# Last norm of a two-layer decoder step: part of its scaling on GpSimd, one tile's on ScalarE, and the samples' last weights taken one product earlier

## The chip, the cores and the metric

The kernel is one program on one core of a Trainium2 chip. The metric is the device time of one execution in microseconds. The engines are TensorE (PE in the profile; PEld is its weight load), VectorE (DVE), ScalarE (ACT), GpSimd (POOL) and SyncE (SP, which only issues transfers); 16 DMA engines move data, whoever issues the transfer.

## The reference

One inference step of a two-layer decoder: a gated linear attention layer and a differential attention layer, each followed by a squared-ReLU feed-forward block, with a layer norm behind every residual sum. There are 1024 new prompt tokens (16 meta tokens go ahead of them) and 8 running sequences with one token each, the "samples". Width 1024, hidden width 4096, all float32.

```
def layer_norm(x, g, b):
    mu = jnp.mean(x, axis=-1, keepdims=True)
    xc = x - mu
    var = jnp.mean(xc * xc, axis=-1, keepdims=True)
    return xc * lax.rsqrt(var + LN_EPS) * g + b
def post_norm(x, f, g, b):
    return layer_norm(DEEPNORM_ALPHA * x + f, g, b)
def sq_relu_mlp(x, w1, w2):
    h = jax.nn.relu(x @ w1)
    return (h * h) @ w2
# the last step of layer 1; y_prompt is x_p without its 16 meta rows, y_sample is x_s
x_p = post_norm(x_p, sq_relu_mlp(x_p, mlp_w1[1], mlp_w2[1]), ln_mlp_g[1], ln_mlp_b[1])
x_s = post_norm(x_s, sq_relu_mlp(x_s, mlp_w1[1], mlp_w2[1]), ln_mlp_g[1], ln_mlp_b[1])
```

## The kernel before

Only the end of the kernel matters here: the feed-forward block of the second layer (`mlp1`) and the norm behind it (`normalize`, `last`).

The 1024 prompt tokens are 8 tiles of 128 rows, held in `Y` (tile t is `Yt[:, t, :]`). The block runs over four groups `g` of 1024 hidden units. Each group has an up part (x times w1) and a down part (hidden times w2), and each part multiplies 2x2 blocks by Strassen's scheme with seven products, numbered 1 to 7. The last group's down part takes its products in the order 1, 5, 6, 7, 4, 3, 2. Each float32 product is three matmuls on a high and a low part: `XH` and its low half (left operand, split by ACT at L202 and VectorE at L203), `whi` and `wlo` (weights, split by ACT at L1528 and GpSimd at L1529). A product is four tiles of 12 matmuls of 512 columns (L206 to L208), into the PSUM buffers `axt` and `mmt`. VectorE adds each result into `RP` or `Y` (`down_tile`, L1600). Operands of the next product are prepared during tile 2 of the present one. Where a product's weight is a sum of two blocks, SP loads the first and GpSimd issues an adding transfer of the second on top (L1525, L1527). Weight slabs of 128x512 go through the tile pools `rw` (five buffers) and `raw` (two), and a fixed buffer `RW`.

The samples' tokens are multiplied beside this. Where a raw weight block is needed, `beside` multiplies a slab with `hs` (the samples' hidden values) into one of two PSUM accumulators (L1547), four slabs for each of four blocks; a slab that the product itself does not have raw is loaded once more (L1533). `beside.quarter` says which block belongs to which product. When all are done, `samples_out` adds residuals and norms the samples (`s_ln`, L667 to L688: sums by TensorE, the rest by VectorE, logarithm and exponential by ACT at L679 and L680), transposes back (L1482) and stores `y_sample`.

The last products finish Y: product 7 and 4 tiles 4 to 7, products 3 and 2 tiles 0 to 3. `normalize` takes each half tile's statistics on VectorE (L990, L994), raises the variance to -1/2 on GpSimd (L999), and ACT scales and shifts the tile in place (L1005). Then `last` applies the norm's scale row `fg` and shift row `fb` (both in the tile called XR):

- Tiles 0, 1 and 4 to 7: VectorE multiplies by `fg` (L1453). The shift rows have been written to the output earlier (L1651, from SP), and GpSimd issues a store of 512 KB that adds to them (L1454).
- Tiles 2 and 3: no ACT. VectorE does each half in two steps, (y - mean) * fg (L1458) and y * rstd + fb (L1459), and SP stores the half, 256 KB, directly (L1460).

The source sets dependences only; a scheduler writes each engine's instruction order when the program is built, and each engine runs its own in that order and waits at semaphores. So an instruction that waits holds everything behind it on its engine.

Of the kernel before, what the change touches and what calls it, by code (L numbers as in the profile page):

```python
# [16 lines left out]
ALU = mybir.AluOpType  # L17
# [5 lines left out]
D = 1024  # L23
# [91 lines left out]
def hybrid_step(ctx, tc, A, dbg=None, upto=9):  # L115
    nc = tc.nc
    V, S, G, TE = nc.vector, nc.scalar, nc.gpsimd, nc.tensor
# [867 lines left out]
    def normalize(steps, stats, done, last=None):  # L985

        st, mv, rs = stats
        half = set()
        for t, j in steps:
            V.bn_stats(st[:, t, j, :], Yt[:, t, j * 512 : (j + 1) * 512])  # L990
            if t not in half:
                half.add(t)
                continue
            V.bn_aggr(mv[:, t, :], st[:, t])  # L994
            if t % 2 == 0 and not last:
                continue
            ts = slice(t if last else t - 1, t + 1)
            V.tensor_scalar(rs[:, 0, ts], mv[:, ts, 1], EPS, None, ALU.add)
            steps_g.append(G.tensor_tensor(rs[:, 0, ts], rs[:, 0, ts], mhalf[:, : ts.stop - ts.start], op=ALU.pow).ins)  # L999
            if last and t in (2, 3):  # L1000
                last(t, mv, rs)
                continue
            V.scalar_tensor_tensor(rs[:, 1, ts], mv[:, ts, 0], -1.0, rs[:, 0, ts], ALU.mult, ALU.mult)
            for x in range(ts.start, ts.stop):
                S.activation(Yt[:, x, :], Yt[:, x, :], AF.Identity, bias=rs[:, 1, x : x + 1], scale=rs[:, 0, x : x + 1])  # L1005
            if last:
                last(t, mv, rs)
            if t % 4 == 3:
                done(t // 4)
# [401 lines left out]
    def rawt():  # L1411
        return rwp.tile([P, 512], F32, name="rw")
# [36 lines left out]
    def last(t, mv, rs):  # L1449

        y, out = Yt[:, t, :], A["y_prompt"][0, t * P : (t + 1) * P, :]
        if t not in (2, 3):
            V.tensor_tensor(y, y, fg, op=ALU.mult)  # L1453
            nc.gpsimd.dma_start(out, y, accum_op=ALU.add)  # L1454
            return
        for h in range(2):
            c = slice(512 * h, 512 * h + 512)
            V.scalar_tensor_tensor(y[:, c], y[:, c], mv[:, t, 0:1], fg[:, c], ALU.subtract, ALU.mult)  # L1458
            V.scalar_tensor_tensor(y[:, c], y[:, c], rs[:, 0, t : t + 1], fb[:, c], ALU.mult, ALU.add)  # L1459
            dma(out[:, c], y[:, c])  # L1460
# [48 lines left out]
    def weight_operand(terms, quarter, side=None):  # L1509

        hi, lo = (wsp.tile([P, 2048], F32R, name=n).rearrange("p (k n) -> p k n", n=512) for n in ("whi", "wlo"))
        run = terms[0] == "run"

        def src(q, k):
            w, r0, c0 = quarter(*q)
            return w[r0 + k * P : r0 + (k + 1) * P, c0 : c0 + 512]

        for k in range(4):
            if run or (len(terms) > 1 and terms[-1] != "new"):
                t = RW[:, k, :]  # L1520
            else:
                count[1] += 1
                t = wrp.tile([P, 512], F32, name="raw") if count[1] % 7 in (0, 3) else rawt()
            if not run:
                loads.append(dma(t, src(terms[0], k)).ins)  # L1525
            if len(terms) > 1:
                nc.gpsimd.dma_start(t, src(terms[1], k), accum_op=ALU.add)  # L1527
            S.copy(hi[:, k, :], t)  # L1528
            G.tensor_tensor(lo[:, k, :], t, hi[:, k, :].bitcast(F32), op=ALU.subtract)  # L1529
            if side:  # L1530
                if terms != [side.quarter]:
                    t = rawt()
                    dma(t, src(side.quarter, k))  # L1533
                side(k, t)
        return hi, lo

    w1, w2 = A["mlp_w1"][1], A["mlp_w2"][1]
# [1 line left out]
    def operands(g, up, i):  # L1539
        if up:  # L1540
            left = weight_operand(UP_W[i], lambda h, k: (w1, 512 * k, 1024 * g + 512 * h))
            right = chip_operand(UP_X[i], lambda k, c: xr(c)[:, 4 * k : 4 * k + 4, :], TH, RX)
            return left, right

        def beside(k, t):
            r, u = beside.quarter
            TE.matmul(acc[u][k * TS : (k + 1) * TS, :], hs[:, 4 * r + k, :], t, start=g == 0 and i in (1, 3), stop=g == 3 and r == 1)  # L1547


        beside.quarter = ({1: (0, 0), 3: (1, 1), 7: (0, 1), 2: (1, 0)} if g < 3 else {1: (0, 0), 5: (0, 1), 6: (1, 0), 7: (1, 1)}).get(i)  # L1550
        left = chip_operand(DOWN_H[i], lambda c, k: HF[:, 4 * k : 4 * k + 4, c, :512], 512, XF[0][:, : 4 * TH] if g == 3 and i == 7 else RX)
        right = weight_operand(DOWN_W[i], lambda k, u: (w2, 1024 * g + 512 * k, 512 * u), beside if beside.quarter else None)
        return left, right

    def hidden(h, c, m):
# [57 lines left out]
    def mlp1():  # L1613
# [6 lines left out]
        for at, (g, up, i) in enumerate(seq):  # L1620
            now = nxt
            if not up and i == 1:
                if g == 0:
                    beta = alpha_row(A["ln_mix_b"][1:2], ALU.add)
                else:
                    for _ in range(2):
                        next(beta, None)
            for t in range(4):
                if t == 2 and at + 1 < len(seq):
                    nxt = operands(*seq[at + 1])  # L1630
                if up:
# [12 lines left out]
            if g == 3 and not up and i == 7:  # L1644
                samples_out()
            if g == 3 and up and i == 7:
                for x, nm in ((fg, "g"), (fb, "b")):
                    dma(x, A["ln_mlp_" + nm][1:2].broadcast_to([P, D]))
                with tc.issue_after(loads[-1]):
                    for t0, t1 in ((0, 2), (4, 8)):  # L1650
                        dma(A["y_prompt"][0, t0 * P : t1 * P], A["ln_mlp_b"][1:2].broadcast_to([(t1 - t0) * P, D]))  # L1651
                spare.extend(XF[0][:, 4 * TH + 512 * j : 4 * TH + 512 * (j + 1)] for j in range(4))

# [30 lines left out]
```

## Time and profile before

| | |
|---|---|
| runs (us) | 2838.25, 2839.62, 2833.88; median 2838.25 |
| span of the profiled execution (first to last instruction) | 2828.8 us |
| device time of the profiled execution | not among the times shown; the median is 9.45 us above the span |
| busy: PE, PEld, DVE, ACT, POOL | 2735.8, 2242.1, 1937.3, 1084.4, 1115.2 us |
| share of the span | 97%, 79%, 68%, 38%, 39% |
| granted TensorE clock, mean | 0.989 |
| DMA | 562.81 MB, mean 199 GB/s |

TensorE is busy 97% of the span, so a change far from TensorE can count only where TensorE waits or has finished. Busy shares are means over the whole span; the end of the kernel must be read by itself, from stretches of the timeline in microseconds since the span's start.

### The profile page before, as it was taken

The page shows a single profiled execution, that of the slowest core. Times are in us where ns is not written, and L with a number is a line of the kernel's source. Part 1 is how long each engine was busy: PE and PEld are TensorE (multiplying, and loading weights), DVE is VectorE, ACT ScalarE, POOL GpSimd, SP SyncE. Part 2 cuts the span into 40 slices and gives each one's busy share as a digit, 9 for nine tenths or more (in the row PEclk, how much of TensorE's full clock was granted, in tenths as well). Part 3 has the DMA queues.
Part 4 walks back from the last instruction along what each step waited for, and adds up shares of the span by engine and source line. Part 5 has one row for each costly group of instructions (what it writes and reads, how often), then busy time and mean ns, then how long its engine had stood idle before and what let it go on. Part 6 is the DMA issues. An engine that isn't in the chain of part 4 may idle for free. (4 is left out here: it accounts for less than half of the span.)

```text
span 2828.8 us, 52247 instructions
## 1 busy us (share of the span) xinstructions
PE 2735.8 (97%) x19849; PEld 2242.1 (79%) x19849; DVE 1937.3 (68%) x3045; ACT 1084.4 (38%) x2221; POOL 1115.2 (39%) x744
## 2 busy tenths in 40 slices
PE   8999989999999999999999999999999999999997
PEld 5866668997777777777798988777898889797985
DVE  4364462568887787778568730877548878978788
ACT  4323343252221222221242112777535546355553
POOL 1142112334344343434234322100026767677764
PEclk9999999999999999999999999999999999999999
DMA  5568751725898898988658995122144555555683
GB/s 197 193 218 272 265 187 50 249 92 166 287 345 301 313 357 294 342 312 316 239 184 306 357 370 166 54 68 65 39 120 94 115 129 116 132 120 117 134 190 86
DMA packets 272552, 562.81 MB, mean 199 GB/s; under 512 B 23510, under 2 KB 140316, under 8 KB 268204
## 3 DMA queue, kind: packets, MB, share of 16 engines
q1 hardware_dynamic: 253004, 522.75, 53.8%
q0 software_dynamic: 19296, 36.71, 8.1%
q8 instruction: 156, 2.56, 0.4%
q14 instruction: 96, 0.79, 0.1%
HBM read 533.00 MB, written 29.52 MB: 199 GB/s over the span
## 5 line engine op out<-in xcount | busy, mean ns | idle before, releaser
L194 POOL TENSOR_TENSOR wlo<-raw,whi 128x512 fp32r<-128x512 f32 x256 | 379.1, 1495 | 727.2 <-ACT whi L193 589.2
L207 PE MATMUL mmt<-wlo,XH 128*128 128x256 f32 (+1 forms) x1760 | 523.4, 299 | 1.3 <-POOL wlo L194 1.3
L206 PE MATMUL mmt<-whi,XH 128*128 128x256 f32 (+1 forms) x1760 | 523.1, 300 | 1.3 <-DVE ast L1244 0.9
L206 PE MATMUL mmt<-XH,whi 128*128 128x512 f32 (+1 forms) x1216 | 435.3, 359 | 6.8 <-DVE Y L967 3.0
L208 PE MATMUL mmt<-whi,XL 128*128 128x256 f32 x1536 | 433.1, 285 | 0.0
L208 PE MATMUL mmt<-XH,wlo 128*128 128x512 f32 (+1 forms) x1216 | 432.5, 356 | 0.0
L193 ACT CAST whi<-raw 128x512 fp32r<-128x512 f32 x256 | 153.3, 620 | 574.3 <-PE mmt L208 184.9
L857 DVE TENSOR_REDUCE sc<-pg 128x16 f32<-128x1024 f32 x256 | 308.3, 1211 | 70.4 <-POOL pg L856 67.9
L207 PEld LDWEIGHTS mmt<-wlo,XH 128*128 128x128 f32 x1760 | 332.5, 189 | 24.8 <-issue 11.8
L206 PEld LDWEIGHTS mmt<-whi,XH 128*128 128x128 f32 x1760 | 330.8, 189 | 24.6 <-issue 11.8
L207 PE MATMUL mmt<-XL,whi 128*128 128x512 f32 x768 | 306.8, 399 | 0.0
L856 DVE TENSOR_TENSOR pg<-pg,qb 128x1024 f32<-128x1024 f32 x192 | 261.2, 1367 | 65.2 <-DMA pg<-in_cache_k 52.8
L208 PEld LDWEIGHTS mmt<-whi,XL 128*128 128x128 f32 x1536 | 288.8, 189 | 6.5 <-issue 5.8
L206 PEld LDWEIGHTS mmt<-XH,whi 128*128 128x128 f32 x1216 | 230.0, 189 | 49.4 <-issue 7.6
L856 POOL TENSOR_TENSOR pg<-pg,qb 128x1024 f32<-128x1024 f32 x64 | 161.3, 2522 | 260.2 <-DMA pg<-in_cache_k 174.3
L208 PEld LDWEIGHTS mmt<-XH,wlo 128*128 128x128 f32 x1216 | 230.0, 189 | 36.6 <-issue 4.1
L206 PE MATMUL mmt<-whi,HH 128*128 128x512 f32 x512 | 204.7, 401 | 3.9 <-DVE Y L1081 3.6
L208 PE MATMUL mmt<-whi,HL 128*128 128x512 f32 x512 | 203.9, 398 | 0.0
L207 PE MATMUL mmt<-wlo,HH 128*128 128x512 f32 x512 | 203.4, 397 | 0.0
L1529 POOL TENSOR_TENSOR wlo<-rw,whi 128x512 fp32r<-128x512 f32 x92 | 156.5, 1737 | 81.6 <-ACT whi L1528 80.2
L1529 POOL TENSOR_TENSOR wlo<-RW,whi 128x512 fp32r<-128x512 f32 x96 | 169.7, 1798 | 47.3 <-ACT whi L1528 47.2
L207 PEld LDWEIGHTS mmt<-XL,whi 128*128 128x128 f32 x768 | 145.4, 189 | 37.2 <-issue 5.5
(431 smaller groups left out, 5673.8 us busy)
## 6 DMA issues: line engine op xcount, KB each, us to landing
pg<-in_cache_k SPq DMA_DIRECT2D x256, 512.0 KB
pg<-in_cache_v SPq DMA_DIRECT2D x256, 512.0 KB
raw<-in_mlp_w SPq DMA_DIRECT2D x164, 256.0 KB
swt<-in_mlp_w SPq DMA_DIRECT2D x32, 1024.0 KB
rw<-in_mlp_w SPq DMA_DIRECT2D x116, 256.0 KB
RW<-in_mlp_w POOLq DMA_DIRECT2D x96, 256.0 KB, 5.9
raw<-in_gla_w_in SPq DMA_DIRECT2D x48, 256.0 KB
swt<-in_gla_w_in SPq DMA_DIRECT2D x12, 1024.0 KB
```

The costliest lines, as they stand in the source:

```text
L193: S.copy(hi[:, c], raw)
L194: G.tensor_tensor(lo[:, c], raw, hi[:, c].bitcast(F32), op=ALU.subtract)
L206: TE.matmul(ps, ah, bh, start=first, stop=False)
L207: TE.matmul(ps, ah, bl, start=False, stop=False)
L208: return TE.matmul(ps, al, bh, start=False, stop=last)
L856: eng.tensor_tensor(pg, pg, qb, op=ALU.mult)
L857: return V.tensor_reduce(sc[:, n, :], pg.rearrange("p (h d) -> p h d", d=64), op=ALU.add, axis=AX.X).ins
L1529: G.tensor_tensor(lo[:, k, :], t, hi[:, k, :].bitcast(F32), op=ALU.subtract)
```

## The change

It does three things. Tiles 0 and 1: the multiplication by `fg` goes from VectorE to GpSimd, in two halves of 512 columns each. Tile 2 now goes the way of the other tiles: ACT scales and shifts it, VectorE multiplies it by `fg` in one piece, and GpSimd issues an adding store, so its output rows are filled with the shift row as well (three tiles instead of two in the first fill). Only tile 3 keeps the two-step form. And in the last group, the samples' block (1, 0) is taken beside product 5 (with block (0, 1)) instead of 6, and block (1, 1) beside 6 instead of 7; `samples_out` is written behind product 6 instead of 7.

```
-            if last and t in (2, 3):
+            if last and t == 3:
                 last(t, mv, rs)
                 continue
...
     def last(t, mv, rs):
         y, out = Yt[:, t, :], A["y_prompt"][0, t * P : (t + 1) * P, :]
-        if t not in (2, 3):
-            V.tensor_tensor(y, y, fg, op=ALU.mult)
+        if t != 3:
+            eng = G if t < 2 else V
+            for h in range(2 if t < 2 else 1):
+                c = slice(512 * h, 512 * h + 512) if t < 2 else slice(0, D)
+                eng.tensor_tensor(y[:, c], y[:, c], fg[:, c], op=ALU.mult)
             nc.gpsimd.dma_start(out, y, accum_op=ALU.add)
             return
...
             if side:
-                if terms != [side.quarter]:
-                    t = rawt()
-                    dma(t, src(side.quarter, k))
-                side(k, t)
+                for q in side.quarters:
+                    if terms != [q]:
+                        t = rawt()
+                        dma(t, src(q, k))
+                    side(k, t, *q)
...
-        beside.quarter = ({...} if g < 3 else {1: (0, 0), 5: (0, 1), 6: (1, 0), 7: (1, 1)}).get(i)
+        beside.quarters = ({...} if g < 3 else {1: [(0, 0)], 5: [(0, 1), (1, 0)], 6: [(1, 1)]}).get(i)
...
-            if g == 3 and not up and i == 7:
+            if g == 3 and not up and i == 6:
                 samples_out()
...
-                    for t0, t1 in ((0, 2), (4, 8)):
+                    for t0, t1 in ((0, 3), (4, 8)):
                         dma(A["y_prompt"][0, t0 * P : t1 * P], A["ln_mlp_b"][1:2].broadcast_to([(t1 - t0) * P, D]))
```

Three lines more in the file move later line numbers by 3 (L1547 becomes L1550, L1454 becomes L1457, the multiplication L1453 becomes L1456). What the scheduler makes of it, at three places. First SP's queue in the last group's down part; `rw` and `raw` are weight slabs, L1533 (now L1537) the slabs for the samples alone, L1525 (now L1528) those for the products. Before:

```order
L1533 DMA rw<-in_mlp_w 128x512 x4
L1525 DMA rw<-in_mlp_w 128x512
L1533 DMA rw<-in_mlp_w 128x512
L1525 DMA rw<-in_mlp_w 128x512
L1533 DMA rw<-in_mlp_w 128x512 x2
L1525 DMA rw<-in_mlp_w 128x512
L1525 DMA raw<-in_mlp_w 128x512
L1533 DMA rw<-in_mlp_w 128x512
L1525 DMA rw<-in_mlp_w 128x512 x6
```

and after:

```order
L1537 DMA rw<-in_mlp_w 128x512 x2
L1528 DMA raw<-in_mlp_w 128x512
L1537 DMA rw<-in_mlp_w 128x512 x8
L1528 DMA rw<-in_mlp_w 128x512 x6
L1528 DMA raw<-in_mlp_w 128x512
```

The samples' slabs all stand ahead of product 7's three `rw` slabs now, where they stood between and behind them.

Second, the end of GpSimd's queue (`brs` is the variance raised to -1/2, XR the row `fg`). Before:

```order
L1454 DMA out_y_prompt<-Y 128x1024
L999 TENSOR_TENSOR brs<-brs,mhalf 128x1
L1454 DMA out_y_prompt<-Y 128x1024
L999 TENSOR_TENSOR brs<-brs,mhalf 128x1 x3
L1454 DMA out_y_prompt<-Y 128x1024 x2
L999 TENSOR_TENSOR brs<-brs,mhalf 128x1
```

and after:

```order
L1457 DMA out_y_prompt<-Y 128x1024 x2
L999 TENSOR_TENSOR brs<-brs,mhalf 128x1 x2
L1456 TENSOR_TENSOR Y<-Y,XR_25166 128x512 x2
L999 TENSOR_TENSOR brs<-brs,mhalf 128x1
L1456 TENSOR_TENSOR Y<-Y,XR_25166 128x512 x2
L1457 DMA out_y_prompt<-Y 128x1024
L999 TENSOR_TENSOR brs<-brs,mhalf 128x1
L1457 DMA out_y_prompt<-Y 128x1024 x2
```

The four half multiplications stand ahead of tile 0's store, with the power of tile 2 between them; the power of tile 3 stands ahead of tile 1's store, and tile 2's store is last.

Third, the end of TensorE's queue: tiles 2 and 3 of product 2 and the samples' eight transposes. Before, the transposes come last:

```order
L206 MATMUL mmt<-whi,XH_86 128x512
L207 MATMUL mmt<-wlo,XH_86 128x512
L208 MATMUL mmt<-whi,XH_24059 128x512
L1482 MATMUL smt<-c_ident,sx 32x128 x8
L1680 UNCONDITIONAL_BRANCH
```

and after, they have 15 matmuls behind them, of which these are the first:

```order
L208 MATMUL axt<-whi,XH_24059 128x512
L1485 MATMUL smt<-c_ident,sx 32x128 x8
L206 MATMUL axt<-whi,XH_86 128x512
L207 MATMUL axt<-wlo,XH_86 128x512
L208 MATMUL axt<-whi,XH_24059 128x512
L206 MATMUL mmt<-whi,XH_86 128x512
```

The three matmuls that end tile 2, and all of tile 3, now follow the samples' transposes.

More of the change, by code (lines that the diff above doesn't have):

```diff
@@ L1543, in operands, with beside @@
             return left, right
-        def beside(k, t):
-            r, u = beside.quarter
+        def beside(k, t, r, u):
             TE.matmul(acc[u][k * TS : (k + 1) * TS, :], hs[:, 4 * r + k, :], t, start=g == 0 and i in (1, 3), stop=g == 3 and r == 1)
-        beside.quarter = ({1: (0, 0), 3: (1, 1), 7: (0, 1), 2: (1, 0)} if g < 3 else {1: (0, 0), 5: (0, 1), 6: (1, 0), 7: (1, 1)}).get(i)
+        beside.quarters = ({1: [(0, 0)], 3: [(1, 1)], 7: [(0, 1)], 2: [(1, 0)]} if g < 3 else {1: [(0, 0)], 5: [(0, 1), (1, 0)], 6: [(1, 1)]}).get(i)
         left = chip_operand(DOWN_H[i], lambda c, k: HF[:, 4 * k : 4 * k + 4, c, :512], 512, XF[0][:, : 4 * TH] if g == 3 and i == 7 else RX)
-        right = weight_operand(DOWN_W[i], lambda k, u: (w2, 1024 * g + 512 * k, 512 * u), beside if beside.quarter else None)
+        right = weight_operand(DOWN_W[i], lambda k, u: (w2, 1024 * g + 512 * k, 512 * u), beside if beside.quarters else None)
         return left, right
```

## The prediction

> **What bounds the kernel now.** I read the busy time by stage first, then what each engine waited for in the last 90 us, then the timeline of the engines that wait, and last what the DMA engines do while the results are stored. Before the last feed-forward stage nothing changes, so I look from 2740 us on. Each row of the first fence gives a stretch of the span, then the busy time (and instruction count) of PE, PE's weight load, DVE, ACT and POOL, the granted clock, the busy share of the 16 DMA engines, and GB/s.
>
> ```profile
> 2740.00:2760.00 20.00, 19.46 (x88) 13.62 (x87) 18.84 (x18) 4.98 (x7) 12.16 (x12) 1.00 0.80 184
> 2760.00:2780.00 20.00, 18.35 (x80) 13.79 (x79) 15.94 (x17) 9.26 (x14) 14.09 (x9) 1.00 0.22 76
> 2780.00:2800.00 20.00, 18.90 (x84) 15.05 (x83) 19.99 (x40) 7.60 (x9) 7.89 (x8) 1.00 0.17 26
> 2800.00:2811.00 11.00, 10.55 (x47) 8.28 (x45) 9.63 (x24) 1.48 (x3) 5.00 (x7) 1.00 0.73 117
> 2811.00:2822.00 11.00, 1.03 (x8) 0.70 (x8) 10.90 (x24) 3.31 (x4) 4.74 (x6) 0.69 0.54 99
> 2822.00:2828.80 6.80, 0.00 (x0) 0.00 (x0) 0.63 (x1) 0.00 (x0) 0.00 (x0) 0.50 0.73 198
> ...
> DVE XH L203 <- ACT XH L202: 7.4, 2, 5.0
> DVE Y L1453 <- ACT Y L1005: 1.4, 1, 1.4
> ...
> PE axt L206 <- DVE sz L1475: 1.1, 1, 1.1
> PE axt L206 <- DVE RP L1600: 1.0, 1, 1.0
> PE axt L207 <- POOL wlo L1529: 0.6, 1, 0.6
> PE smt L1547 <- DMA rw<-in_mlp_w: 0.5, 1, 0.5
> ```
>
> Up to 2811 TensorE is nearly full (it loses 1.1 + 1.0 + 0.6 + 0.5 = 3.2 us to waits); from 2780 VectorE is full as well; after 2811 only VectorE works; after 2822 only the DMA engines. The wait rows are all that these two engines had from 2740 on (us in total, times, longest). The next fence is the timeline: start, duration, engine, line, and in brackets the idle time before it and what ended it.
>
> ```profile
> 2762.36 0.62 ACT L1528 CAST whi<-rw 128x512 fp32r<-128x512 f32 x1 [8.00 <-DMA rw<-in_mlp_w]
> 2762.88 1.99 ACT L202 CAST XH<-HF 128x1024 fp32r<-128x1024 f32 x2
> ...
> 2763.96 1.46 DVE L203 TENSOR_TENSOR XH<-HF,XH 128x1024 fp32r<-128x1024 f32 x1 [5.02 <-ACT XH L202]
> ...
> 2803.12 0.67 DVE L1600 TENSOR_TENSOR Y<-Y,mmt 128x512 f32<-128x512 f32 x1
> ...
> 2806.52 1.23 DVE L1453 TENSOR_TENSOR Y<-Y,XR 128x1024 f32<-128x1024 f32 x1 [1.36 <-ACT Y L1005]
> ...
> 2821.22 1.41 DVE L1459 SCALAR_TENSOR_TENSOR Y<-Y,brs,XR 128x512 f32<-128x512 f32 x2
> ```
>
> The reader sees a chain of queues. ACT waits 8.00 us for the fourth weight slab of product 7; the split of the left operand stands behind it in ACT's queue; so VectorE sits idle for 5.02 us, and from 2763.96 to 2803.75 (39.8 us, until the last sum of product 3 is in Y) it never idles again. It has fallen behind TensorE there and stays behind until the end.
>
> **The change, part by part.** *Samples' weights one product ahead.* Loads 9 to 12 of the side products leave the stretch in which product 7's weights are loaded. I let product 7's weights come in time, and then ACT's split waits only for TensorE to have read the left operand's old half, some six matmuls into product 6's last tile.
>
> ```profile
> 2740.05 1.07 PE L1547 MATMUL smt<-rw,hs 128*32 128x512 f32 x8
> ...
> 2755.99 0.39 PE L208 MATMUL axt<-whi,XH 128*128 128x512 f32 x1
> ...
> 2799.04 0.40 PE L206 MATMUL axt<-whi,XH 128*128 128x512 f32 x1
> ...
> 2810.16 0.40 PE L208 MATMUL mmt<-whi,XH 128*128 128x512 f32 x1
> ```
>
> Tile 2 of product 6 ends at 2756.4 (the L208 row of 2755.99). One of the 16 side products, 1.07/4 = 0.27 us, now stands ahead of that place: 2756.65. Product 2, 48 matmuls, takes 2799.04 to 2810.39, or 0.236 us a matmul, so six take 1.4: 2758.05. ACT's split is half of 1.99, some 1.05: VectorE starts at 2759.1 where it started at 2763.96. That is a gain of 4.8 us; its bounds are 0 (the weights are late all the same) and 4.8. The eight loads of product 5's side work in five buffers are costed at nothing: the first of them that must wait for a buffer is used some 24 matmuls, 5.7 us, after it is freed, and a 256 KB load took 3.7 us. Without that cover TensorE would lose the difference, up to 3 us.
>
> ```profile
> 2755.77 0.33 SPq L1533 DMA_DIRECT2D rw<-in_mlp_w  x1
> ...
> 2759.47 1.04 PE L1547 MATMUL smt<-rw,hs 128*32 128x512 f32 x2 [0.54 <-DMA rw<-in_mlp_w]
> ```
>
> VectorE then has the same 39.8 us of work up to product 3's last sum, plus the samples' steps that now come before it: L686, 0.41 or less, and five small ones like L683, some 0.1 each where the next instruction starts before they end, 0.85 us in all (rows below). So 2759.1 + 39.8 + 0.85 = 2799.8, against 2803.75. The 1.36 us wait goes: the samples' logarithm, which held ACT's queue there, now stands before ACT's split for product 2.
>
> ```profile
> 2803.72 1.27 DVE L990 BATCH_NORM_STATS2 bst<-Y 128x6 f32<-128x512 f32 x2
> ...
> 2808.36 0.18 DVE L683 TENSOR_TENSOR sv__31477<-sv__31477,sy__31478 128x32 f32<-128x32 f32 x1
> ...
> 2810.64 0.41 DVE L686 TENSOR_TENSOR sz<-sz,sy__31478 128x256 f32<-128x256 f32 x1
> ...
> 2815.27 1.22 DVE L1453 TENSOR_TENSOR Y<-Y,XR 128x1024 f32<-128x1024 f32 x1
> ```
>
> *TensorE's queue.* The samples' eight transposes now stand before the last 15 matmuls. They wait for VectorE's last sample step, which comes two statistics (0.6 each) and two steps of 0.33 after product 3's last sum: 2801.8. TensorE, rid of its 3.2 us of waits but kept about 1 us by POOL's last split of product 2 (its ACT cast stands behind the samples' logarithm, which waits for VectorE), is there at about 2802.9. Cover: 1.1 us; beyond that every us of VectorE's delay is one of TensorE's. TensorE ends near 2807.7 instead of 2810.55, which is not on the path.
>
> *The last norm.* From 2801.8 VectorE multiplies tile 7 (1.14 us), adds and measures tiles 0 and 1 (four times 0.6, and 0.25 for two or three small steps like L683): tile 0's variance is there at 2805.6. Then POOL's power (0.55 to 0.6), VectorE's 0.1, ACT's scaling (half of 2.37): 2807.5. Here POOL takes over:
>
> ```profile
> 2796.76 2.27 POOL L1529 TENSOR_TENSOR wlo<-raw,whi 128x512 fp32r<-128x512 f32 x1
> 2798.99 1.29 POOL L1529 TENSOR_TENSOR wlo<-rw,whi 128x512 fp32r<-128x512 f32 x1
> ...
> 2800.84 1.68 POOL L1529 TENSOR_TENSOR wlo<-rw,whi 128x512 fp32r<-128x512 f32 x1
> ...
> 2810.82 1.18 POOL L999 TENSOR_TENSOR brs<-brs,mhalf 128x1 f32<-128x1 f32 x2 [1.89 <-DVE brs L998]
> ...
> 2812.16 2.37 ACT L1005 ACTIVATE Y<-Y,brs 128x1024 f32<-128x1024 f32 x2 [5.55 <-DVE brs L1003]
> ```
>
> POOL's queue is: two halves of tile 0, the power of tile 2, two halves of tile 1, and only then tile 0's store. No multiplication by POOL stands at this place in the trace; the nearest is its subtraction of the same shape, 1.29 (VectorE on sums and statistics) to 2.27 us (VectorE on subtractions of two SBUF tensors). I take 1.29 for tile 0 and 1.68 for tile 1, beside which VectorE has its L1461 steps: 2 x 1.29 + 0.6 + 2 x 1.68 = 6.55, so 2814.05. Bounds: 5.75 and 9.7. The Trainium skill, "SBUF — State Buffer", section "Who interferes with whom", says that a tensor_tensor of VectorE with both inputs in SBUF and a GpSimd instruction exclude each other for a whole instruction. The 2.27 us row agrees with it and the 1.29 us row, taken beside VectorE's sums out of PSUM, does not contradict it; by that rule tile 1's halves, beside L1461, would take 2.27 each, POOL would be through at 2815.2 and the gain found below would be 0 instead of 1.2 us.
>
> VectorE loses in this stretch two multiplications (2 x 1.14) and tile 2's four half steps (two take 1.41 or less, start to start 0.66 each), and gains tile 2's one (1.14): 3.8 us less. It ends near 2816, when POOL's power of tile 3 has come, instead of 2821.96. If the stores did not bind, that would be the gain.
>
> *The stores.* Rows by stretch, as in the first fence (an adding store alone, two of them, then the last six stores), and the stores on the queues:
>
> ```profile
> 2795.00:2800.00 5.00, 5.00 (x24) 4.03 (x23) 5.00 (x8) 1.56 (x2) 5.00 (x4) 1.00 0.67 105
> 2801.00:2808.00 7.00, 7.00 (x32) 5.68 (x31) 5.63 (x13) 1.48 (x3) 2.93 (x4) 1.00 0.90 153
> 2818.00:2827.20 9.20, 0.00 (x0) 0.00 (x0) 4.56 (x9) 0.00 (x0) 1.86 (x2) 0.50 0.99 228
> ...
> 2794.37 0.90 POOL L1454 DMA_DIRECT2D out_y_prompt<-Y  x1 [1.73 <-ACT whi L1528]
> ...
> 2816.78 0.89 POOL L1454 DMA_DIRECT2D out_y_prompt<-Y  x1 [2.29 <-DVE Y L1453]
> ...
> DMA to landing us min/median/max: 5.2/5.8/7.9
> ```
>
> One adding store of 512 KB occupies all 16 DMA engines for 0.67 x 5 = 3.35 us, two for 6.3; I take 3.2 each. The last stretch holds two adding and four direct stores: 9.1 us, so a direct half tile is (9.1 - 6.4) / 4 = 0.68. The DMA engines are full there, from 2818 to 2827.05: this is what ends the kernel. After the change three adding and two direct stores remain, 3 x 3.2 + 2 x 0.68 = 10.95 us, and they cannot start before POOL is through: 2814.05 + 0.85 from issue to first bytes + 10.95 = 2825.85. That is 1.2 us before 2827.05. The start moves from 2816.78 to 2814.05, but the work behind it grows by 1.85.
>
> **The sum.** The span would be 2827.6 against 2828.8. The device time of that one execution is not shown; the median of the three runs, 2838.25, is 9.45 above its span, and I keep that distance: 2837.0. Its bounds, with POOL at 5.75 or 9.7 and VectorE 1 us either way: 2835 to 2841.5. Whatever is within 0.2%, 5.7 us, I call the same, which is what runs spread over 5.7 us can tell.
>
> **Rivals.** (A) The stores overlap and only the last counts. POOL issues tile 2's store at 2815.9; with the shortest landing, 5.2, it ends at 2821.1, 5.95 us earlier: 2832.3. For it: VectorE really ends 6 us earlier. Against: two stores issued 2.3 us apart needed 6.3 us of full engines. (B) Slower: three adding stores queued at once do not overlap at all, and each takes its median landing, 5.8: 2814.05 + 17.4 + 1.36 = 2832.8, which is 5.75 later, 2844.0. It decides as soon as a queued store costs more than 3.6 us. For it: the longest landing, 7.9. Against: the same 6.3 us for two. (C) The first part does not do what it says: product 7's weights, or TensorE, stall elsewhere, and VectorE starts as late as before. Then POOL starts 4.8 us later and everything ends at 2830.65, 3.6 later: 2841.85. For it: DMA is 0.80 busy from 2740 to 2760 and the twelve loads crowd into what comes just before. Against: TensorE has 24 matmuls of cover.
>
> **How the numbers follow.** My sum 0.62, A 0.16, B 0.07, C 0.12, something unseen 0.03. The time is that of the sum, 2837.0. The range goes from A to just short of B, 2831.8 to 2843.0; the sum's own is 2835 to 2841.5. Faster by over 0.2%: A, which lies at that bound, and a little scatter, 0.16; slower: B and a little of C, 0.08; the rest 0.76.
>
> **What would show it.** Right: ACT's 8 us wait and VectorE's 5 us wait are gone; POOL's multiplications take 1.3 to 1.7 us and tile 0's store is issued near 2814; VectorE ends near 2816 but the DMA engines are full for about 11 us up to some 2 us before the end. Wrong: if the DMA engines idle between the three stores, or if VectorE still waits for ACT near 2760, or if TensorE stands at the samples' transposes for more than 2 us.

## The result, and the profile after

The changed kernel is slower. Its 13 runs have a median of 2844.58 us, those of the kernel before on the same chip 2837.18; the ratio is 1.0025 with a 95% interval of 1.0015 to 1.0036, or 7.4 us (4.3 to 10.2). The profiled execution took 2844.68 us with a span of 2842.7, so what lies around the span is 1.9 us; in the runs on record it is 1.7 to 2.5 us.

Both traces must first be put on one clock. But for the one tile more that is filled with the shift row, the code ahead of the last group's down part is the same in both, yet its first 128x512 matmul of product 1 starts at another time. From the timeline of before, and then of after (start, duration, engine, line):

```profile
2722.07 0.39 PE L206 MATMUL axt<-whi,XH 128*128 128x512 f32 x1
```

```profile
2727.70 0.39 PE L206 MATMUL axt<-whi,XH 128*128 128x512 f32 x1
```

5.63 us of the 13.9 between the spans were there before the parts that I want to compare. I call this matmul's start zero, and give times from it as "at 41.9" from here on. The end of the span is at 106.7 before and at 115.0 after: 8.3 us, and that agrees with the 7.4 of the medians. Over all the profiles below, zero itself lies anywhere from 2721.8 to 2737.7; that is the spread of the runs, and a difference of a few us between two spans means nothing without this step.

The timeline after, the rows that answer to those of before:

```profile
2765.21 0.62 ACT L1531 CAST whi<-rw 128x512 fp32r<-128x512 f32 x1 [4.07 <-DMA rw<-in_mlp_w]
2766.79 0.62 ACT L1531 CAST whi<-rw 128x512 fp32r<-128x512 f32 x1 [0.96 <-DMA rw<-in_mlp_w]
2768.71 1.05 ACT L202 CAST XH<-HF 128x1024 fp32r<-128x1024 f32 x1 [1.29 <-PE mmt L207]
2769.79 1.23 DVE L203 TENSOR_TENSOR XH<-HF,XH 128x1024 fp32r<-128x1024 f32 x1 [0.45 <-ACT XH L202]
...
2814.47 0.68 DVE L1603 TENSOR_TENSOR Y<-Y,mmt 128x512 f32<-128x512 f32 x1
...
2821.77 1.24 ACT L1005 ACTIVATE Y<-Y,brs 128x1024 f32<-128x1024 f32 x1 [3.35 <-DVE brs L1003]
...
2823.09 2.49 POOL L1456 TENSOR_TENSOR Y<-Y,XR 128x512 f32<-128x512 f32 x2 [1.02 <-ACT Y L1005]
2825.54 0.55 POOL L999 TENSOR_TENSOR brs<-brs,mhalf 128x1 f32<-128x1 f32 x1
2826.05 2.48 POOL L1456 TENSOR_TENSOR Y<-Y,XR 128x512 f32<-128x512 f32 x2
2828.47 0.86 POOL L1457 DMA_DIRECT2D out_y_prompt<-Y  x1
...
2830.81 1.40 DVE L1462 SCALAR_TENSOR_TENSOR Y<-Y,brs,XR 128x512 f32<-128x512 f32 x2
```

The long waits are gone, ACT's 8.00 us and VectorE's 5.02. But VectorE's split for product 7 starts at 2769.79, which is at 42.09, where it started at 41.89: what was waited for by ACT is now waited for elsewhere. Product 3's last sum ends at 87.45 instead of 81.72. Tile 0's store is issued at 100.77 instead of 94.71. The end of the span by stretches (busy PE, PEld, DVE, ACT, POOL, the granted clock, DMA share, GB/s):

```profile
2822.00:2828.00 6.00, 0.00 (x0) 0.00 (x0) 4.95 (x11) 3.25 (x4) 4.97 (x6) 0.80 0.19 37
2828.00:2830.00 2.00, 0.00 (x0) 0.00 (x0) 2.00 (x3) 0.61 (x1) 2.00 (x3) 0.50 0.29 25
2830.00:2839.60 9.60, 0.00 (x0) 0.00 (x0) 2.21 (x3) 0.00 (x0) 1.86 (x3) 0.50 1.01 210
2839.60:2842.70 3.10, 0.00 (x0) 0.00 (x0) 0.00 (x0) 0.00 (x0) 0.00 (x0) 0.50 0.03 10
```

For 6 us the DMA engines do a fifth of what they could, while GpSimd multiplies; from 2830 they are full for 9.6 us; then 3.1 us pass in which next to nothing is busy (1.75 before). The full stretch near the end was predicted, but for its place on the clock.

Where TensorE lost its time is in the samples' matmuls. After (before, the rows were `x8`, `x8`, `x6`, `x2`; a slab leaves two records, so eight are the four slabs of a block):

```profile
2733.35 1.92 PE L1550 MATMUL smt<-rw,hs 128*32 128x512 f32 x10
2740.73 1.05 PE L1550 MATMUL smt<-rw,hs 128*32 128x512 f32 x2
2743.29 1.04 PE L1550 MATMUL smt<-rw,hs 128*32 128x512 f32 x2
2744.93 1.05 PE L1550 MATMUL smt<-rw,hs 128*32 128x512 f32 x2
2750.04 1.05 PE L1550 MATMUL smt<-rw,hs 128*32 128x512 f32 x4
2751.45 1.04 PE L1550 MATMUL smt<-rw,hs 128*32 128x512 f32 x2
2753.32 1.04 PE L1550 MATMUL smt<-rw,hs 128*32 128x512 f32 x2
```

One slab alone (`x2`) takes 1.05 us; four in a row took 1.07. They write 32 partitions each, in four different quarters of the accumulator. The Trainium skill, "TensorEngine Tiling (Array Packing)", section "Tiling Modes", says that with 32 columns the array works as four independent tiles; the two rows, 1.07 for four and 1.05 for one, agree with it. Slabs that come one at a time use one tile of the four, so eight groups (the `x10` row holds a group of four and a slab by itself) now stand ahead of product 6 where there were two, and product 6 starts at 31.33 instead of 24.63.

### The profile page after: what moved, and what is told of

It reads as the page before. It is cut to its first block, busy times and chain, and to the rows that moved or that the text cites. A ratio compares the mean times of both kernels' runs of the same rounds, so it can differ in the third digit from the quotient of the medians.

```text
span 2842.7 us, 52247 instructions
## 1 busy us (share of the span) xinstructions
PE 2737.5 (96%) x19849; PEld 2238.8 (79%) x19849; DVE 1941.1 (68%) x3041; ACT 1084.1 (38%) x2222; POOL 1118.4 (39%) x749
## 5 line engine op out<-in xcount | busy, mean ns | idle before, releaser
L194 POOL TENSOR_TENSOR wlo<-raw,whi 128x512 fp32r<-128x512 f32 x256 | 371.7, 1466 | 744.0 <-ACT whi L193 644.2
L856 DVE TENSOR_TENSOR pg<-pg,qb 128x1024 f32<-128x1024 f32 x192 | 255.0, 1335 | 65.2 <-DMA pg<-in_cache_k 58.9
```

Of the source, the lines that this page charges most:

```text
L194: G.tensor_tensor(lo[:, c], raw, hi[:, c].bitcast(F32), op=ALU.subtract)
L856: eng.tensor_tensor(pg, pg, qb, op=ALU.mult)
```

## The experiments

All times are from zero, in us, out of one profile each: the start of VectorE's split for product 7, the issue of tile 0's store (by GpSimd), VectorE's end, and the end of the span, "whole". The ratio to before is that of the timed runs.

| kernel | split 7 | store | VectorE | whole | ratio, 95% interval |
|---|---|---|---|---|---|
| before | 41.89 | 94.71 | 100.56 | 106.73 | |
| before_again | 42.77 | 95.61 | 101.46 | 107.86 | 0.9997, 0.9988 to 1.0007 |
| after | 42.09 | 100.77 | 104.51 | 115.00 | 1.0025, 1.0015 to 1.0036 |
| norm_only | 43.89 | 99.99 | 102.18 | 115.35 | 1.0027, 1.0016 to 1.0039 |
| samples_only | 42.09 | 96.88 | 105.12 | 108.63 | 1.0008, 0.9996 to 1.0021 |
| apart | 47.79 | 100.66 | 106.51 | 112.74 | 1.0024, 1.0009 to 1.0039 |
| grouped | 39.71 | 110.86 | 113.93 | 126.21 | 1.0068, 1.0048 to 1.0089 |
| pool_only | 41.66 | 97.97 | 101.22 | 109.45 | 1.0011, 0.9996 to 1.0026 |
| tile2_only | 43.20 | 94.29 | 100.25 | 107.45 | 1.0004, 0.9992 to 1.0016 |
| norm_early | 43.53 | 95.98 | 104.37 | 112.78 | 1.0026, 1.0012 to 1.0039 |
| after_early | 42.08 | 98.20 | 106.58 | 115.30 | 1.0027, 1.0017 to 1.0037 |
| vector_mult | 42.09 | 96.89 | 104.01 | 111.96 | 1.0037, 1.0023 to 1.0051 |
| vector_mult_again | 42.09 | 96.86 | 103.98 | 111.91 | 1.0014, 1.0002 to 1.0027 |
| no_slabs | 37.52 | 91.95 | 99.71 | 103.54 | 0.9980, 0.9965 to 0.9995 |
| no_slabs_norm | 36.85 | 94.14 | 97.86 | 108.28 | 1.0011, 0.9996 to 1.0025 |
| tile1_direct | 42.10 | 94.95 | 101.87 | 105.58 | 0.9989, 0.9976 to 1.0001 |
| tile1_again | 43.24 | 96.08 | 103.00 | 106.80 | 0.9986, 0.9973 to 1.0000 |
| tiles01_direct | 43.75 | direct | 104.73 | 107.82 | 0.9997, 0.9985 to 1.0009 |
| own_first | 37.77 | 91.82 | 97.66 | 103.74 | 0.9993, 0.9981 to 1.0005 |
| own_first_tile1 | 37.76 | 91.80 | 98.72 | 102.60 | 0.9977, 0.9963 to 0.9991 |

In the kernels that load in the old order the split varies from 41.7 to 43.9 (apart, where TensorE is late, has 47.8), with the moment at which a slab arrives; a difference of a microsecond or two in "whole" can be that. So I also compare from the split to the end, which is 64.8 and 65.1 us in the two profiles of before.

**The change in its two parts.** From the two traces alone I held that the samples' part had cost 5.7 us (product 3's last sum) and the norm's part 2.5 (from there to the end). norm_only is the kernel before with the first, second and last hunk of the diff, samples_only with the others.

> The kernel before with the last norm's part of the change alone (tiles 0 and 1 multiplied by GpSimd in halves, tile 2 by ScalarE and an adding store); the samples as before. I measure from product 1's first matmul in the last group's down part to the end of the span: 106.7 us in the profile of before, 115.0 in that of the changed kernel. Theory: the stretch from product 3's last sum to the end was 25.7 us before and 28.2 after, and that difference belongs to this part, so 108.7 to 111 here, +2 to +5 us in time; product 7's split and product 3's last sum stay where they were (41.9 and 81.7 us from product 1's first matmul). Rival: the norm's part costs nothing by itself and all of the loss is the samples': 106.7, within 1 us, or less.

> The kernel before with the samples' part alone (block (1, 0) beside product 5, (1, 1) beside 6, samples' output behind 6); the norm as before. Theory: TensorE goes from product 1's first matmul to product 6's first in 31.3 us as in the changed kernel instead of 24.6, since it multiplies the samples' slabs in eight groups there instead of two, at 1.1 us a group whether one slab or four; product 3's last sum comes 4 to 6 us later; the whole stretch takes 110 to 112.5 us instead of 106.7, +3.5 to +6 us in time. Rival: the samples' part is neutral and the norm's part cost all: 106.7 within 1 us. What I had predicted for it: 3 to 4 us earlier at product 3's last sum.

It is the other way round; both missed what I expected. The norm's part alone costs most of it: 115.35 against 106.7 and 107.9, and 1.0027. Up to 2 us of that are its late split; from the split to the end it needs 71.5 us, 6.5 more than before. The samples' part alone costs 1 to 2 us, 66.5 from the split to the end, although TensorE and VectorE's last sum are as late in it as in the changed kernel (31.33 and 87.45). VectorE's end at 105.1 costs little there; the two adding stores had been issued by 98.6, and direct half tiles remain. By the column "whole" the two costs seem not to add (8.6 and 1.9 alone, 8.3 together, by the first profile). From the split they do: 6.5 and 1.6 alone, 7.9 together (72.9 in the changed kernel, 65.0 before). Splitting a difference of two traces at a milestone had put it into the wrong part.

**Is it the isolated slabs, or slabs not loaded?** apart has the loads and the order of before, and forces TensorE's order alone:

```
...
+            # after every third matmul of the third tile: one of the four slabs
+            if pend and t == 2:
+                side, kk, x = pend.pop(0)
+                with tc.issue_after(m.ins):
+                    slab = side(kk, x)
```

> The kernel before, with the same loads in the same order, but the four slabs of block (0, 1) and the four of (1, 0) are multiplied one at a time with three matmuls of the product between them, where they were multiplied four in a row. Theory (a slab alone costs TensorE what four in a row cost, some 1.05 us): six groups more, so product 1's first matmul to product 6's first takes 24.6 + 6.3 = 30.9 us (30 to 32); since VectorE's split for product 7 waits for weights until 41.9 us, up to 6 us of it is hidden at the end: 0 to +5 us. Rival (TensorE lost that time to slabs that had not been loaded, which five buffers for eight slabs bring about): the stretch stays at 24.6 to 25.5 us and the time within 1 us, since these slabs were there.

The stretch from zero to product 6, first in before, then in apart:

```profile
2722.07:2746.70 24.63, 24.63 (x115) 18.18 (x114) 20.34 (x17) 15.36 (x28) 20.39 (x19) 1.00 0.73 166
```

```profile
2728.46:2760.11 31.65, 31.65 (x115) 18.50 (x114) 25.00 (x22) 15.03 (x28) 21.11 (x19) 1.00 0.63 133
```

The same 115 instructions of TensorE, 7.0 us more. So it is the isolation, at 1.17 us for each of six groups. Less of it was hidden than the theory said: the split came at 47.79, since the loads moved back with TensorE, and the whole grew by 5 to 6; from the split to the end it is 64.95, as before.

grouped is the changed kernel with each block's slabs multiplied four in a row at fixed places (`{(1,2): (0,1), (5,2): (1,0), (6,1): (1,1)}`, product and tile to block):

> The changed kernel, but the slabs of block (0, 1) are multiplied as a group ahead of product 1's third tile, those of (1, 0) four in a row ahead of product 5's third tile and those of (1, 1) ahead of product 6's second. The eight loads and five buffers stay. Theory (groups cost, not loads): product 1's first matmul to product 6's first takes 25.5 to 27 us instead of 31.3, product 3's last sum comes 3 to 5 us earlier than in the changed kernel, the whole stretch takes 110 to 112 us instead of 115.0. Rival (loads): TensorE then waits for the slabs in a row, the stretch to product 6 stays near 31 us and the whole at 114 to 116.

Its first part held: product 6 starts at 26.89 and the split comes at 39.71. The whole, 126.2, was far off, from a cause that neither theory had. GpSimd's six subtractions came in one run, and VectorE's split waited for them all; then VectorE's queue stood for a matmul that TensorE's queue held back. VectorE's and then GpSimd's timeline:

```profile
2768.69 8.33 DVE L203 TENSOR_TENSOR XH<-HF,XH 128x1024 fp32r<-128x1024 f32 x1
...
2788.09 0.19 DVE L678 TENSOR_SCALAR sv__31391<-smt 128x32 f32<-128x32 f32 x1 [7.21 <-PE smt L675]
```

```profile
2767.83 5.63 POOL L1532 TENSOR_TENSOR wlo<-RW,whi 128x512 fp32r<-128x512 f32 x4
2772.82 3.10 POOL L1532 TENSOR_TENSOR wlo<-rw,whi 128x512 fp32r<-128x512 f32 x2
```

A split of 1.23 us took 8.33, and it ended 1.1 us after GpSimd's last subtraction. The time of grouped says nothing on the samples' part, then.

**The norm's part in pieces.** pool_only: `eng = G if t < 2`, tile 2 as before. tile2_only: `t == 3` in place of `t in (2, 3)`, VectorE multiplies all.

> The kernel before, with tiles 0 and 1 multiplied by GpSimd in halves and nothing else: tile 2 keeps its two steps and direct stores, so the DMA work is as before. Times from product 1's first matmul; the whole was 106.7 us before, 115.35 with the whole norm part. Theory (the norm part costs because the first of the last stores is issued late): tile 0 is scaled at 91.3 us as before, then GpSimd needs 2.5 us for its halves, 1 us for a power that waits, 2.6 us for tile 1's halves, all ahead of tile 0's store, which so is issued at 97 to 98.5 us instead of 94.7; then 6.4 us of adding stores at least and 3 us from the last byte to the end where an adding store is last: whole 108 to 111, +1.5 to +4 us in time. Rival (the third adding store alone costs): 106.7 within 1 us.

> The kernel before, with tile 2 alone changed: ScalarE scales it, VectorE multiplies it in one piece, GpSimd issues an adding store; tiles 0 and 1 stay on VectorE. Times from product 1's first matmul. Theory: tile 0's store is issued at 94.7 us or up to 1.3 earlier (a pair of half steps less ahead of it on VectorE), the last stores need 10.95 us of all DMA engines instead of 9.1, and an adding store that lands last ends the span 3.0 us after the last byte instead of 1.8: whole 108.5 to 110 against 106.7, +2 to +3.5 us in time. Rival (only GpSimd's four multiplications ahead of the store cost): 105.5 to 107, since VectorE has less to do.

GpSimd's halves alone put the store back to 97.97 and the whole to 109.45, as expected: 1.6 to 2.7 us. Tile 2's adding store alone costs less than expected, nothing that can be told: the first store starts at 94.3, with less for VectorE to do ahead of it, and the 1.85 us of additional transfers do not show at the end. From the split to the end the two are 2.8 us more and 0.7 less than before, but together, in norm_only, 6.5 more. I read that as three adding stores that queue behind a first one at 100; no run isolates this. Two orders of GpSimd's queue, on norm_only and on the changed kernel:

```
+            with tc.issue_after(stores[-2]) if last and t in (2, 3) else nullcontext():
                 steps_g.append(G.tensor_tensor(rs[:, 0, ts], ..., op=ALU.pow).ins)
...
+                with tc.issue_after(stores[-1]) if t == 1 else nullcontext():
                     eng.tensor_tensor(y[:, c], y[:, c], fg[:, c], op=ALU.mult)
```

> The whole norm part, samples as before, but GpSimd's queue is written as tile 0's halves, tile 0's store, tile 1's halves, power of tile 2, tile 1's store, power of tile 3, tile 2's store; in the norm part alone tile 0's store stood behind all four halves and both powers, at 100.0 us from product 1's first matmul. Theory: tile 0's store is issued at 94 to 96, the DMA engines have the same 10.95 us of work but begin 4 to 6 us earlier, and may idle between the stores: whole 109.5 to 112.5 instead of 115.35, a time 3 to 6 us under that of the norm part alone, still 2 to 6 us over before. Rival (the place of tile 0's store does not matter, the end is set by the last store, tile 2's, behind ScalarE and VectorE): 114 to 116.

> The changed kernel with GpSimd's queue written as tile 0's halves, tile 0's store, tile 1's halves, power of tile 2, tile 1's store, power of tile 3, tile 2's store. Theory: tile 0's store is issued at about 98 us from product 1's first matmul instead of 100.8, the DMA engines begin 2.8 us earlier, and tile 2's store is issued at 103 to 105 as before; whole 112 to 114 instead of 115.0. Rival (only the last store counts): 114.5 to 116.

The first lies just above its range in the profile (112.8), and its time did not fall as expected (1.0026 against 1.0027). The second is a miss (115.3), as its rival said: tile 0's store does go out 2.6 us earlier, but the end does not follow. Two of GpSimd's rows in after_early, tile 0's store and tile 2's:

```profile
2827.00 0.89 POOL L1459 DMA_DIRECT2D out_y_prompt<-Y  x1 [0.30 <-POOL Y L1458]
...
2835.01 0.89 POOL L1459 DMA_DIRECT2D out_y_prompt<-Y  x1 [2.22 <-DVE Y L1458]
```

Tile 2's store now waits for VectorE, which multiplies tile 2 late, and its issue at 106.2 is 2.7 later than in the changed kernel. So two bounds seem to lie close together: the start of the first store with all transfers behind it, and an adding store that is issued at VectorE's end. From that issue to the end of the span it is 7.6 to 9.1 us (vector_mult 104.31 to 111.96, after_early 106.21 to 115.30), from VectorE's end with a direct half tile last only 3.1 to 3.9 (tiles01_direct 3.1, own_first_tile1 3.9).

vector_mult undoes GpSimd's multiplications in the changed kernel (`V.tensor_tensor(y, y, fg, op=ALU.mult)` for all):

> The changed kernel with one part undone: VectorE multiplies tiles 0 and 1 again; tile 2's adding store and the samples' part stay. Theory (GpSimd's halves ahead of the first store cost most): tile 0's store is issued at about 97 us from product 1's first matmul as in the samples' part alone, instead of 100.8; VectorE multiplies tile 2 last, near 104, and its store ends the span, so 110 to 112 us instead of 115.0, 3 to 5 us of time less than the changed kernel. Rival (VectorE is late by the samples' part, and the end follows it whoever multiplies): 114 to 117.

> The changed kernel with VectorE's multiplications of tiles 0 and 1 put back, once more, since its profile (112.0 us from product 1's first matmul, 3.0 less than the changed kernel) and its five times (0.37% over before) said different things. Theory: again 111 to 113, and a time 0.1 to 0.25% over before. Rival (something ahead of this stretch is slower in that program): 111 to 113 and again 0.3% or more.

The profiles gave 111.96 and 111.91, as expected, 3 us less than the changed kernel. The times leave it open: five gave 1.0037, twelve more 1.0014 (1.0002 to 1.0027), and the changed kernel's 1.0025 lies between.

**The lead by itself.** no_slabs leaves out the samples' last four slabs (`7: (1, 1)` is gone), no_slabs_norm adds the norm's part to that.

> The kernel before without the last four slabs of the samples (block (1, 1) of the last group): neither loaded nor multiplied, so y_sample lacks their part; all else as before. Times from product 1's first matmul. Theory (my prediction's first two steps hold in themselves): product 7's weights come in time, VectorE starts its split at about 37 us instead of 41.9 and keeps the lead: product 3's last sum at 77 to 79 instead of 81.7; the whole 102.5 to 104.5 instead of 106.7 to 107.9, 3 to 5 us less time. Rival (the lead is lost again to TensorE or to GpSimd's lock): last sum at 80.5 to 82, whole 106 to 108.

> The same without those four slabs, and with the norm's part of the change; GpSimd's queue ends as in the changed kernel. My prediction's sum with the full lead: whole 105.5 us from product 1's first matmul. Theory as it stands now: tile 0's store is issued at 94.5 to 96.5, then 1.2 us to the first bytes, 10 to 11 us of DMA work and 3 us from the last byte to the end: 109 to 111.5, 5 to 8 us more than without the norm's part.

With nothing in the way of product 7's weights the split starts at 36.9 to 37.5, where the prediction had put it, and 3 to 4 us of that remain at the end, 0.9980. Half of the theory missed: product 3's last sum comes at 82.77, no earlier than before, as the rival had it. One of VectorE's multiplications, 1.2 us elsewhere, took 6.76 and ended 1.1 us after the last of GpSimd's subtractions. VectorE's row and the last of GpSimd's in no_slabs:

```profile
2806.27 6.76 DVE L1453 TENSOR_TENSOR Y<-Y,XR 128x1024 f32<-128x1024 f32 x1
```

```profile
2809.14 2.80 POOL L1529 TENSOR_TENSOR wlo<-rw,whi 128x512 fp32r<-128x512 f32 x2
```

Tile 0's store still left 2.8 to 3.7 us earlier than before, since less stood behind that sum. The norm's part on top of it costs 4.7 us: 108.28, less than the 109 to 111.5 expected, where the prediction's sum is 105.5. Given the lead, then, the change would at best have been about even (1.0011, 0.9996 to 1.0025), by a lead of 3 to 4 us against a norm's part that costs 4.7.

**The other direction.** If the last stores bind, fewer adding stores should help: tile 1, then tiles 0 and 1, get the shift row from VectorE and go out directly (and their rows are left out of the first fill).

```
             V.tensor_tensor(y, y, fg, op=ALU.mult)
+            if t == 1:
+                for h in range(2):
+                    c = slice(512 * h, 512 * h + 512)
+                    V.tensor_tensor(y[:, c], y[:, c], fb[:, c], op=ALU.add)
+                    dma(out[:, c], y[:, c])
+                return
```

> The opposite of the change, on the kernel before: tile 1 no longer has an adding store; VectorE adds the shift row in two halves (1.2 us more on VectorE) and SP stores each half directly, so the last stores are one adding and six direct ones, 3.2 + 6 x 0.68 = 7.3 us of all DMA engines instead of 9.1. Theory (the end is bound by the DMA engines, VectorE has 2 to 3 us to spare there): 1 to 2 us less than before's 106.7 from product 1's first matmul, 104.7 to 106; too little for the time to tell apart. Rival (VectorE sets the end): 1 to 1.5 us more, 107.7 to 108.2.

> The kernel that stores tile 1 directly, with one adding store among the last instead of two, once more. Theory: 105 to 106.5 us from product 1's first matmul against 106.7 and 107.9 of before; a time 1 to 3 us less than before. Rival: no difference from before.

> One step further than the kernel that stores tile 1 directly (105.6 us from product 1's first matmul): tiles 0 and 1 both get their shift row by VectorE and direct stores, so eight direct half tiles and no adding store among the last. Theory: the DMA work falls to 5.4 us, but VectorE has 2.4 us more than before and ends near 103; it now sets the end, 3.5 us behind its last instruction: 106 to 107, no better than storing tile 1 alone so. Rival (still bound by the DMA engines): 103.5 to 104.5.

> The kernel before once more, for a second profile: how steady the measure from product 1's first matmul to the end of the span is (106.7 us in the first). All theories: 106 to 109, with product 7 starting between 38.5 and 42 us as its last weights come; the time as before.

From the split to the end it is 63.5 and 63.6 us with tile 1 direct, 64.8 and 65.1 before: 1.4 us, and the ratios 0.9989 and 0.9986 say the same, with intervals that just reach 1. The second profile's 106.80 lies above its range, with a split at 43.24. With both tiles direct nothing is gained: VectorE ends last, at 104.73, and the whole is 107.82, above the 106 to 107 expected, with a split at 43.75.

Last, the lead without leaving anything out: in the last group product 7's own slabs are loaded ahead of the samples' (1, 1) slabs, in the same five buffers; and that with tile 1 direct.

```
+            if side and not side.late:      # late: last group, product 7
...
+        if side and side.late:              # behind the loop over product 7's own slabs
+            for k in range(4):
+                t = rawt()
+                with tc.issue_after(loads[-1]):
+                    dma(t, src(side.quarter, k))
+                side(k, t)
```

> The kernel before, but in the last group product 7's three own slabs are loaded ahead of the samples' slabs of block (1, 1) instead of between them; nothing left out, norm as before. Times from product 1's first matmul. Theory (the order of loads held product 7's split): split at 36.8 to 39 us instead of 41.9 to 42.8, whole 103.5 to 106 instead of 106.7 to 107.9, 1 to 4 us less time. Rival (the samples' slabs now come late, TensorE waits for them ahead of product 7): product 7 starts at 41 or later, whole 106 to 108.5.

> The same, and tile 1 stored directly (VectorE adds its shift row, 1.3 us less by itself between product 7's split and the end). Theory: whole 102.5 to 105, a time 0.1 to 0.2% under before. Rival: product 7 starts at 41 or later, whole 104.5 to 107.

Both do what was expected in the profile, 103.74 and 102.60, and in own_first the last sum comes at 78.84. own_first's times do not separate it from before, own_first_tile1 is faster than the kernel before: 0.9977 (0.9963 to 0.9991), 6.5 us. Its end, for comparison with that of the changed kernel above:

```profile
2825.00:2828.00 3.00, 0.00 (x0) 0.00 (x0) 3.00 (x5) 0.00 (x0) 0.79 (x1) 0.50 0.75 122
2828.00:2833.80 5.80, 0.00 (x0) 0.00 (x0) 3.78 (x8) 0.00 (x0) 0.99 (x1) 0.50 0.95 292
2833.80:2835.70 1.90, 0.00 (x0) 0.00 (x0) 0.00 (x0) 0.00 (x0) 0.00 (x0) 0.50 0.05 20
```

VectorE and the DMA engines end within 2 us of each other, and 1.9 us later the span ends.

## Why the prediction was wrong, by its own steps

- **The frame.** "The median is 9.45 above its span, and I keep that distance": what lies around the span is some 2 us. The profiled execution was a quick one, some 6.5 us under the median. This moved no difference, since it was added to both sides.
- **Samples' weights one product ahead: the step that failed.** The gain was put at 4.8 us with bounds 0 and 4.8; it was -0.2. The weights came in time, as it said, but "one of the 16 side products, 1.07/4 = 0.27 us" priced a slab alone at a quarter of a group, and it costs the whole group (apart). "The eight loads of product 5's side work in five buffers are costed at nothing" looked at whether TensorE would wait for a load. It did not: no wait for a slab stands among TensorE's waits. The built order has slabs multiplied one at a time, and that was the price, 6.7 us up to product 6. TensorE's queue, which is fixed when the program is built, has groups of 5, 1, 1, 1, 2, 1, 1 slabs where there were 4, 4, 3, 1.
- **VectorE's 39.8 + 0.85 us to product 3's last sum** were 45.4 (42.09 to 87.45). The samples' small steps were taken from places where GpSimd was idle; here they fall beside its subtractions. VectorE's rows before, then after:

```profile
2784.92 0.48 DVE L1477 SCALAR_TENSOR_TENSOR sz<-sx,sz 128x128 f32<-128x128 f32 x2
...
2808.36 0.18 DVE L683 TENSOR_TENSOR sv__31477<-sv__31477,sy__31478 128x32 f32<-128x32 f32 x1
```

```profile
2775.74 2.69 DVE L1480 SCALAR_TENSOR_TENSOR sz<-sx,sz 128x128 f32<-128x128 f32 x2
...
2802.94 1.23 DVE L683 TENSOR_TENSOR sv__31391<-sv__31391,sy__31392 128x32 f32<-128x32 f32 x1
...
2807.49 0.67 DVE L684 TENSOR_SCALAR sv__31391<-sv__31391 128x32 f32<-128x32 f32 x1
```

  Counted from start to start, the six samples' steps took 2.3 us instead of 0.85; L1480, L672 and L1003 took 4.6 more than the same lines before, the splits and multiplications (L203, L1456) 1.4 more, and the sums of L1603 gave 2.4 back. own_first, with a lead of four us but the samples' steps behind product 7 as before, needed 41.1 us for the stretch.
- **TensorE at the transposes, cover 1.1 us** (by the rows shown nearer 2). It waited 2.1 there, which was one of the signs of being wrong, and 2.3 at another of the samples' matmuls, which had not been looked at:

```profile
PE smt L675 <- DVE ss L673: 2.3, 1, 2.3
PE smt L1485 <- DVE sx L688: 2.1, 1, 2.1
```

- **The last norm** came near its number: from the last sum to the issue of tile 0's store 13.3 us (predicted 14.25), of which GpSimd 5.4 (predicted 6.55, bounds 5.75 to 9.7; all four halves ran at 1.24, and the waits were VectorE's: a L1003 of 1.21 and a pair of L1461 of 2.20). **The stores** did so too: 10.3 us of full DMA engines (10.95; 0.6 of it up to 2830, 9.7 behind). From the issue to the end of the span it was 14.2 us, 13.55 predicted, with 3.1 us instead of 1.75 behind the last byte. That these two fit does not make the norm's part cheap: samples_only, without it, needs 9.4 us to the store and 11.75 behind it, so it adds 3.9 and 2.5 us.
- **The sum of the miss** at tile 0's store: predicted at 92.0, measured at 100.8. Split 5.1 late, VectorE's stretch 4.7 longer, the norm 0.9 shorter. Beside the lead, the price of the rest was too low: the prediction's own sum has 68.5 us from the split to the end, 3.7 more than before; it was 72.9, 8.1 more. By the experiments 6.5 of that are the norm's part and 1.6 the samples'.
- **The rivals.** C is what happened, "TensorE stalls elsewhere, VectorE starts as late as before"; it was held to be unlikely by a cover of 24 matmuls, and its +3.6 left out the 4.4 us more from the split to the end. A and B fell: the stores neither overlapped nor took 5.8 each.

## What to carry to other kernels

Count in the built order how an instruction's neighbours change, not only where it goes: work that is cheap in groups is dear when its inputs come one at a time. When the last transfers bind, ask for the issue of the first of them and for the kind of the last: put nothing on the queue ahead of the one, and let the other be small and direct (after_early moved the first alone, and gained nothing). And put two traces on one clock at the last common instruction before any time is compared, take out what already varied without the change, then check each part of a change by itself; a difference cut at a milestone is not a cause.

## What the runs showed of the hardware

- Four float32 slabs of 32 columns (128x512, two records each), on four quarters of the output's partitions, take 1.07 us when they stand in a row; one alone takes 1.05.
- VectorE with two SBUF inputs can wait behind several of GpSimd's subtractions that come without a gap: a 1.23 us split took 8.33 behind six of them, a 0.18 us step 1.23. It need not wait for all: in the changed kernel a split that started at 2771.93 took 2.19, within a run of four that lasted from 2771.74 to 2778.28. The Trainium skill, "SBUF — State Buffer", section "Who interferes with whom", has the lock for a whole instruction, and the order of issue decides; that VectorE can lose five turns in a row is what these rows add. It goes the other way too: a pair of GpSimd's halves took 2.49 us in the changed kernel and 3.42 in pool_only, where VectorE had its two-step work beside them.
- From the moment at which the share of the DMA engines fell under 0.3 to the end of the span (in steps of 0.2 us) it took 1.4 to 2.2 us where the last adding store was issued 1.6 us or more ahead of VectorE's end, 2.8 to 3.8 where it was issued 1.0 us ahead of it or later. Whether the adding itself or the issue by GpSimd makes the difference, no run tells apart.
